# When a block-sum step's sums are rounded: before or after the next step's load work

## The chip, the cores and the metric

One core of a Trainium2 chip runs the whole kernel. The metric is the device time of one execution in microseconds (us). The engines are TensorE (PE for its matmuls, PEld for its weight loads), VectorE (DVE), ScalarE (ACT), GpSimd (POOL) and SyncE (SP), which issues most DMAs. Each takes its own instructions strictly in the order in which the program holds them, and waits on semaphores for the others.

## What is computed

The reference is a trunk of two residual layers on 256 tokens of 2048 features, all in float32: an attention mixer, then a recurrent mixer, each followed by a gated feed-forward of width 5632. The change touches the feed-forward alone:

```python
def swiglu(h, w_gate, w_up, w_down):
    return (jax.nn.silu(h @ w_gate) * (h @ w_up)) @ w_down

for i in range(DEPTH):          # DEPTH = 2
    ...
    x = x + swiglu(rms_norm(x, norm_ffn[i]), ffn_w_gate[i], ffn_w_up[i], ffn_w_down[i])
```

## The kernel before

**Products of float32.** A float32 operand is split in a rounded part `hi` (type fp32r) and a remainder `lo`, and a product takes three matmuls: hi by hi, hi by lo, lo by hi. Weights come from HBM as float32 tiles `raw`. ACT rounds `raw` to `hi` (L160), DVE subtracts to get `lo` (L164 or L173), and PE multiplies (L351).

**Steps.** `load_step` brings one step's weights, 1 MB: two half tiles of 128 x 1024 each, so its `hi` and its `lo` cost one 128 x 2048 instruction each. A plain step is eight products, 24 matmuls of 512 columns. A block-sum step covers the same part of the product as a plain step with seven products in place of eight, 21 matmuls. For it `load_step(True)` also makes three sums of weight blocks. One quarter of the tile arrives as a sum already, because POOL issues a DMA that adds to what SP's DMA wrote (L157). DVE then forms the others in place in `raw`, first one block (L166, 512 wide), then two (L167, 1024 wide). ACT rounds them to `wth` (L170, 512 and 1024 wide), and DVE takes the remainders `wtl` (L171, the same widths). PE's order in a block-sum step is four products from `hi` and `lo` (12 matmuls), then three from `wth` and `wtl` (9 matmuls). The first of these three takes the last of the three sums, so PE's 13th matmul needs the 1024 wide `wth` and the 14th the 1024 wide `wtl`.

**Groups.** A feed-forward is cut in parts of 12, 16 and 16 blocks of 128 hidden features. Each part has 3 or 4 gate/up units (512 columns of `w_gate` and of `w_up` each), then two pairs of column groups of `w_down`. Each unit or pair is a group of eight steps, called 0 to 7 here (six in the `w_down` pairs of the first part). Steps 1, 3 and 5 are block-sum steps (1 and 3 in the groups of six; 3 and 5 in a layer's first unit, whose steps run in the order 0, 1, 2, 4, 3, 6, 5, 7; none in the second `w_down` pair of layer 0's last part). The program has 93 of them. In a group of eight, steps 6 and 7 are loaded as two halves for each of the two column groups, so that the first column group is done before the second.

**What follows a gate/up unit.** When a unit's sums are done, DVE adds the parts (L851), ACT takes the SiLU (L618), DVE multiplies (L855) and transposes (L868). ACT then copies the 32 x 32 blocks into place with 16 instructions (L874), rounds the result to an operand of the down product (L881), DVE takes the remainder (L882), and where the down product will have a block-sum step there, DVE and ACT prepare its token sums (L333, L336, L337). All of this is queued in `owed`, and is emitted while the next group's steps 1 to 3 are: three pieces after step 1's loading (`settle(3)`).

**What sets the order.** PE's order is the order of the code. For ACT and DVE, `in_line` (L109) ties each engine's load work (L160, L164, L173, L166, L167, L170, L171) in the order in which it is written; a scheduler places the other instructions around it.

**Buffers.** `raw` has 4, `hi` and `lo` have 3 each, `wth` and `wtl` one each. So the rounding of a step waits until PE has finished the step three before it, the rounding of its sums until PE has finished the previous block-sum step, and a step's DMA until DVE is through with the `raw` of the step four before it.

Of the kernel before, what the change touches and what calls it, by code (L numbers as in the profile page):

```python
# [12 lines left out]
F32 = mybir.dt.float32  # L13
F32R = mybir.dt.float32r
AF = mybir.ActivationFunctionType
ALU = mybir.AluOpType
AX = mybir.AxisListType

P = 128
# [13 lines left out]
WIDE = 512  # L33
# [37 lines left out]
def trunk(ctx, tc, w, out):  # L71
    nc = tc.nc
    act, dve, pool, pe, sync = nc.scalar, nc.vector, nc.gpsimd, nc.tensor, nc.sync
# [13 lines left out]
    def nm(s):  # L87
        uid[0] += 1
        return f"{s}_{uid[0]}"
# [8 lines left out]
    def follow(i, j):  # L98
        tc.add_manual_dep(
            i.ins, j.ins.name,  # L100
            mybir.DependencyInfo(mybir.DependencyClass.NoSync, mybir.DependencyReason.DATA),
            reason="order",
        )
        return i
# [4 lines left out]
    def in_line(eng, i):  # L109
        if eng in line:  # L110
            if line[eng] is not None:
                follow(i, line[eng])
            line[eng] = i
        return i
# [6 lines left out]
    def settled(i, n, eng="dve"):  # L121
        for k in [k for k in due if k[0] <= n and k[1] == eng]:
            for j in due.pop(k):
                follow(i, j)

    def load_tiles():
        return [wp.tile([P, 2, HALF, P], dt, tag=t, name=nm(t), bufs=n) for t, dt, n in (("raw", F32, 4), ("hi", F32R, 3), ("lo", F32R, 3))]
# [17 lines left out]
            settled(rest, taken[0] - 1)  # L145
        return [(hi[:, i, :], lo[:, i, :]) for i in range(n)]

    def load_step(seven=False):
        assert taken[0] % 2 == 0
        srcs = [order[taken[0] + i][0] for i in range(2)]  # L150
        taken[0] += 2
        raw, hi, lo = load_tiles()
        if seven:
            for k in (1, 0):
                sl = slice(k * FOUR, k * FOUR + FOUR)
                sync.dma_start(out=square(raw[:, 1, sl, :]), in_=square(srcs[1][:, sl, :]))
            pool.dma_start(out=square(raw[:, 1, FOUR:, :]), in_=square(srcs[1][:, :FOUR, :]), accum_op=ALU.add)  # L157
        for i in range(1 if seven else 2):
            newest["load"] = sync.dma_start(out=raw[:, i], in_=srcs[i])
        newest["cast"] = in_line("act", act.copy(hi, raw))  # L160
        settled(newest["cast"], taken[0] - 1, "act")
        b = [t[:].rearrange("p j (k c) f -> p (j k) (c f)", k=2) for t in (raw, hi, lo)]
        if seven:
            settled(in_line("dve", dve.tensor_tensor(lo, raw, hi[:].bitcast(F32), ALU.subtract)), taken[0] - 1)  # L164
            t = b[0]
            in_line("dve", dve.tensor_tensor(t[:, 0, :], t[:, 3, :], t[:, 0, :], ALU.subtract))  # L166
            in_line("dve", dve.tensor_tensor(t[:, 1:3, :], t[:, 1:3, :], t[:, :1, :].broadcast_to([P, 2, WIDE]), ALU.subtract))  # L167
            th, tl = (fp[1].tile([P, 3, WIDE], F32R, tag=n, name=nm(n), bufs=1) for n in ("wth", "wtl"))
            for sl in (slice(0, 1), slice(1, 3)):
                in_line("act", act.copy(th[:, sl, :], t[:, sl, :]))  # L170
                in_line("dve", dve.tensor_tensor(tl[:, sl, :], t[:, sl, :], th[:, sl, :].bitcast(F32), ALU.subtract))  # L171
        else:
            settled(in_line("dve", dve.tensor_tensor(lo, raw, hi[:].bitcast(F32), ALU.subtract)), taken[0] - 1)  # L173
        w = [(b[1][:, i, :], b[2][:, i, :]) for i in range(4)]
        return w + [(th[:, i, :], tl[:, i, :]) for i in range(3)] if seven else w

    def halves(src, kt):
        return [(src[:, a : min(a + HALF, kt), :], min(HALF, kt - a)) for a in range(0, kt, HALF)]
# [61 lines left out]
    taken = [0]  # L240
# [34 lines left out]
    def step():  # L275
        clock[0] += 1
        due = [i for i, (t, _) in enumerate(waiting) if t <= clock[0]]
        if due:
            waiting.pop(due[0])[1]()
# [8 lines left out]
    def new_accs():  # L288
        return [new_acc() for _ in range(2)]
# [25 lines left out]
    def square(t):  # L315
        return t.rearrange("p c f -> p (c f)")
# [3 lines left out]
    def settle(n=1):  # L320
        while owed and n:
            owed.pop(0)()
            n -= 1
# [16 lines left out]
    def project_pair(xs, forms, plan, middle, done, ready=None, turned=True):  # L340
        banks, spare = [[], []], []
        begun = set()

        def bank(j, a):
            if not banks[j]:
                banks[j].extend(new_accs())
            return banks[j][a]

        def product(acc, x, wt, last=False):
            for i, (a, b) in enumerate(((x[0], wt[0]), (x[0], wt[1]), (x[1], wt[0]))):  # L350
                pe.matmul(acc, a, b, start=id(acc) not in begun, stop=last and i == 2)  # L351
                begun.add(id(acc))
            step()
            step()

        def tokens(k, a):
            return [xs[k][:, o + a * P : o + (a + 1) * P] for o in (0, S)]

        seven = [n for n, cols in plan if n in forms]
        for i, (n, cols) in enumerate(plan):  # L360
            if n in forms:
                s1, s2, s3, s4 = forms[n]
                b11, b21, b22, t3, t2, t4, t1 = load_step(True)
                settle(3)
                if n == seven[0]:
                    p1, q6, q5, q7 = (ps_m.tile([P, WIDE], F32, tag="pm", name=nm("pm")) for _ in range(4))
                last = n == seven[-1]
                product(p1, tokens(2 * n, 0), b11, last)
                product(bank(0, 0), tokens(2 * n + 1, 0), b21)
                product(bank(1, 0), s4, b22)  # L370
                product(q7, s3, t3, last)
                product(q5, s1, t1, last)
                product(q6, s2, t2, last)
                product(bank(0, 1), tokens(2 * n + 1, 1), t4)
                if last:
                    middle(p1, q5, q6, q7)
                continue
            if len(cols) == 1 and i and len(plan[i - 1][1]) == 2:
                settle(-1)
                if ready:  # L380
                    ready()
            end = n == plan[-1][0]
            for j in cols:
                if not spare:
                    w = load_step()
                    spare.extend((w[:2], w[2:]))
                w = spare.pop(0)
                if i:
                    settle(2 if len(owed) > 6 else 1)
                for a in range(2):  # L390
                    for k in range(2):
                        product(bank(j, a), tokens(2 * n + k, a), w[1 - k if turned and j else k], end and k == 1)
                if end:
                    done(j, banks[j])
# [163 lines left out]
    fp = []  # L558
# [16 lines left out]
    def output(xs, norm, ready):  # L575
        def done(c, accs):
            for a, acc in enumerate(accs):
                y = x_tok[:, a, c, :]
                not_after(dve.tensor_tensor(y, y, acc, ALU.add))
            norm.add(c)  # L580

        project_pair(xs, {}, pair_plan(range(KT // 2), READY), None, done, ready, False)
        for c in (2, 3):
            done(c, project_tokens(xs))


    def down(n, xs, forms, norm=None, end=False):
        for c in (0, 2):
            def middle(*banks):
                t = merge(*banks)  # L590
                y = x_tok[:, :, c : c + 2, :].rearrange("p a c f -> p c a f")
                dve.tensor_tensor(y, y, t, ALU.add)

            def done(j, accs):
                for a in range(2):
                    m = 2 if end and c + j == NCOL - 1 else 1
                    for i in range(m):
                        sl = slice(i * WIDE // m, (i + 1) * WIDE // m)
                        y = x_tok[:, a, c + j, sl]
                        not_after(dve.tensor_tensor(y, y, accs[a][:, sl], ALU.add))  # L600
                        if end:
                            sync.dma_start(out=out[:, a, c + j, sl], in_=y)
                if norm is not None:
                    norm.add(c + j)

            alone = norm is not None and c > 0
            project_pair(xs, {} if alone else forms, down_plan(n // 2, alone), middle, done)
# [525 lines left out]
```

## Time and profile before

| | |
|---|---|
| three runs | 2153.76, 2154.16, 2154.3 us; median 2154.16 |
| the profiled execution | 2155.09 us; its span, first to last instruction, 2153.3 us |
| busy over the span | PE 94%, DVE 80%, ACT 62%, POOL 9% |
| DMA | 410.48 MB, mean 191 GB/s |
| mean granted TensorE clock | 0.974 |

In rows of the trace a matmul of 512 columns shows as 0.39 us, but one starts every 0.227 us when PE does not wait, because they are pipelined. PE's busy time therefore hides short waits, and the time between starts tells more. Where a row has a bracket, the engine stood idle before it for so long, and the name behind the arrow ended the wait.

### The profile page before, as it was taken

Reading aid. Unit: us, or ns where it says so; the run is one execution under the profiler, and the core shown is the slowest. Engines: PE = TensorE matmul, PEld = TensorE weight load, DVE = VectorE, ACT = ScalarE, POOL = GpSimd, SP = SyncE. Lnnn points to the kernel's source line nnn. Section 1 sums busy time; section 2 is a strip of 40 time slices with the busy share of each in tenths; the row PEclk is TensorE's granted clock in tenths of the full one; section 3 lists DMA queues with packets and bytes.
Section 4 is the critical chain, followed back from the end, with each engine's and each line's share of the span. In section 5 each row is a group of like instructions: output and inputs, shape, how many; then the busy total and the mean of one; then the engine's idle time right before and its main releaser. Section 6 shows DMA issues by size and latency. Waiting matters only on the chain.

```text
span 2153.3 us, 26372 instructions
## 1 busy us (share of the span) xinstructions
PE 2030.9 (94%) x9641; PEld 1683.1 (78%) x9641; DVE 1724.3 (80%) x1928; ACT 1327.9 (62%) x1803; POOL 185.3 (9%) x240
## 2 busy tenths in 40 slices
PE   9999999899898998889999999998998999988999
PEld 7888877687777886668899998877787777877777
DVE  6777887797777887779888877877787777877778
ACT  6665765645565546667699996665555555555653
POOL 0011000000000000001033420000000000000000
PEclk9999999999999999999999999999999999999999
DMA  9533565576556775666555545656576565766565
GB/s 356 179 138 120 203 190 174 167 217 212 171 174 199 219 219 171 188 180 236 189 172 179 193 140 203 192 181 193 171 226 188 187 190 175 218 189 189 177 194 163
DMA packets 136354, 410.48 MB, mean 191 GB/s; under 512 B 15264, under 2 KB 16160, under 8 KB 135968
## 3 DMA queue, kind: packets, MB, share of 16 engines
q1 hardware_dynamic: 122688, 384.40, 52.2%
q0 software_dynamic: 13392, 24.39, 7.0%
q8 instruction: 75, 1.23, 0.2%
q14 instruction: 55, 0.45, 0.1%
q10 hardware_dynamic: 144, 0.02, 0.0%
HBM read 406.64 MB, written 2.10 MB: 190 GB/s over the span
## 4 chain that ended last, share of the span: by engine, by line
PE 58%; DVE 17%; ACT 16%; issue 6%; DMA 2%; POOL 0%; ACTq 0%; SPq 0%; DVEq 0%; POOLq 0%
PE acc L351 40%; PE acc L300 9%; PE pm L351 6%; ACT hi L160 6%; ACT tf L874 5%; DVE lo L173 3%; DVE raw L167 2%; DVE lo L164 2%; DVE fg L851 1%; DVE fg L855 1%; DVE raw L166 1%; DVE tb L868 1%; ACT L618 1%; ACT wth L170 1%; ACT sg L618 1%
## 5 line engine op out<-in xcount | busy, mean ns | idle before, releaser
L351 PE MATMUL acc<-hi,xg 128*128 128x512 f32 x1920 | 638.9, 404 | 28.0 <-ACT hi L160 28.0
L160 ACT CAST hi<-raw 128x2048 fp32r<-128x2048 f32 x280 | 528.1, 1907 | 139.4 <-DMA raw<-in_w_up_dram 50.0
L173 DVE TENSOR_TENSOR lo<-raw,hi 128x2048 fp32r<-128x2048 f32 x187 | 425.9, 2291 | 148.5 <-ACT hi L160 148.4
L351 PEld LDWEIGHTS acc<-hi,xg 128*128 128x128 f32 x1920 | 377.3, 197 | 114.4 <-ACT hi L160 34.9
L170 ACT CAST wth<-raw 128x512 fp32r<-128x512 f32 (+1 forms) x186 | 155.8, 837 | 442.1 <-DVE raw L166 362.2
L351 PE MATMUL acc<-lo,xg 128*128 128x512 f32 x960 | 392.6, 409 | 37.6 <-DVE lo L173 37.6
L351 PE MATMUL acc<-hi,act 128*128 128x512 f32 x1258 | 411.5, 398 | 11.5 <-ACT hi L160 10.5
L351 PEld LDWEIGHTS acc<-hi,act 128*128 128x128 f32 x1258 | 242.4, 193 | 64.7 <-ACT hi L160 13.1
L351 PE MATMUL acc<-lo,act 128*128 128x512 f32 x629 | 252.5, 401 | 14.2 <-DVE lo L173 14.0
L351 PEld LDWEIGHTS acc<-lo,xg 128*128 128x128 f32 x960 | 188.4, 196 | 89.6 <-DVE lo L173 50.2
L164 DVE TENSOR_TENSOR lo<-raw,hi 128x2048 fp32r<-128x2048 f32 x93 | 212.6, 2286 | 37.2 <-ACT hi L160 37.1
L171 DVE TENSOR_TENSOR wtl<-raw,wth 128x512 fp32r<-128x512 f32 (+1 forms) x186 | 177.4, 955 | 47.0 <-ACT wth L170 47.0
L144 DVE TENSOR_TENSOR lo<-raw,hi 128x1024 fp32r<-128x1024 f32 (+1 forms) x146 | 179.3, 1256 | 30.2 <-ACT hi L142 29.6
L142 ACT CAST hi<-raw 128x1024 fp32r<-128x1024 f32 (+1 forms) x146 | 145.0, 1035 | 41.1 <-PE acc L300 14.8
L351 PEld LDWEIGHTS acc<-lo,act 128*128 128x128 f32 x629 | 121.0, 192 | 44.8 <-DVE lo L173 20.5
L157 POOL DMA_DIRECT2D raw<-in_w_up_dram x64 | 55.5, 867 | 1054.1 <-DMA raw<-in_w_up_dram 911.4
L406 PE MATMUL acc<-xg,hi 128*128 128x256 f32 x512 | 145.6, 284 | 0.0
L407 PE MATMUL acc<-xg,hi 128*128 128x256 f32 x512 | 145.4, 284 | 0.0
L408 PE MATMUL acc<-xg,lo 128*128 128x256 f32 x512 | 145.1, 283 | 0.0
L874 ACT COPY tf<-tb 32x256 f32<-32x256 f32 x352 | 141.6, 402 | 4.1
L167 DVE TENSOR_TENSOR raw<-raw 128x1024 f32<-128x1024 f32 x93 | 113.0, 1215 | 2.4
L300 PE MATMUL acc<-hi,xg 128*128 128x512 f32 x320 | 107.8, 397 | 0.7 <-ACT hi L142 0.7
(208 smaller groups left out, 3162.7 us busy)
## 6 DMA issues: line engine op xcount, KB each, us to landing
raw<-in_w_gate_dram SPq DMA_DIRECT2D x176, 512.0 KB, 4.7
raw<-in_w_down_dram SPq DMA_DIRECT2D x147, 512.0 KB, 5.0
raw<-in_w_up_dram SPq DMA_DIRECT2D x112, 512.0 KB, 4.9
raw<-in_w_up_dram SPq DMA_DIRECT2D x128, 256.0 KB, 3.2
raw<-in_w_in_dram SPq DMA_DIRECT2D x64, 512.0 KB, 4.7
raw<-in_w_qkv_dram SPq DMA_DIRECT2D x46, 512.0 KB, 5.9
raw<-in_w_o_dram SPq DMA_DIRECT2D x32, 512.0 KB, 4.0
raw<-in_w_up_dram POOLq DMA_DIRECT2D x64, 256.0 KB, 6.1
```

The lines of the kernel that those rows point to most:

```text
L144: rest = in_line("dve", dve.tensor_tensor(lo[:, sl, :], raw[:, sl, :], hi[:, sl, :].bitcast(F32), ALU.subtract))
L160: newest["cast"] = in_line("act", act.copy(hi, raw))
L164: settled(in_line("dve", dve.tensor_tensor(lo, raw, hi[:].bitcast(F32), ALU.subtract)), taken[0] - 1)
L167: in_line("dve", dve.tensor_tensor(t[:, 1:3, :], t[:, 1:3, :], t[:, :1, :].broadcast_to([P, 2, WIDE]), ALU.subtract))
L170: in_line("act", act.copy(th[:, sl, :], t[:, sl, :]))
L171: in_line("dve", dve.tensor_tensor(tl[:, sl, :], t[:, sl, :], th[:, sl, :].bitcast(F32), ALU.subtract))
L173: settled(in_line("dve", dve.tensor_tensor(lo, raw, hi[:].bitcast(F32), ALU.subtract)), taken[0] - 1)
L300: pe.matmul(accs[a], x, wt[:, k, :], start=(k0 + k == 0 and n == 0), stop=(end and k == 1 and n == 2))
L351: pe.matmul(acc, a, b, start=id(acc) not in begun, stop=last and i == 2)
L406: pe.matmul(o, hi, x[:, :S], start=start, stop=False)
L407: pe.matmul(o, hi, x[:, S:], start=False, stop=False)
L874: n = act.copy(f[32 * i : 32 * i + 32, q::4, :, :], b[32 * q : 32 * q + 32, :, i, :, :])
```

## The change

`load_step` is split. `begin_step` issues a step's DMAs, its `hi` and its `lo`, and for a block-sum step also the two subtractions in `raw`. The new `load_step`, when it is asked for a block-sum step, first calls `begin_step` for the step behind it and keeps the result in `begun`; only then come the roundings `wth` and the remainders `wtl` of its own sums. No instruction is added or removed. PE's order, and that of the DMAs on SP and POOL, is the same as before; on ACT and on DVE the order differs around each of the 93 block-sum steps.

```diff
+    begun = []
+
+    def begin_step(seven):
...
         newest["cast"] = in_line("act", act.copy(hi, raw))
         settled(newest["cast"], taken[0] - 1, "act")
+        settled(in_line("dve", dve.tensor_tensor(lo, raw, hi[:].bitcast(F32), ALU.subtract)), taken[0] - 1)
...
         if seven:
-            settled(in_line("dve", dve.tensor_tensor(lo, raw, hi[:].bitcast(F32), ALU.subtract)), taken[0] - 1)
             in_line("dve", dve.tensor_tensor(t[:, 0, :], t[:, 3, :], t[:, 0, :], ALU.subtract))
             in_line("dve", dve.tensor_tensor(t[:, 1:3, :], t[:, 1:3, :], t[:, :1, :].broadcast_to([P, 2, WIDE]), ALU.subtract))
+        return t, [(hi[:, i, :], lo[:, i, :]) for i in range(4)]
+
+    def load_step(seven=False, after=False):
+        t, w = begun.pop() if begun else begin_step(seven)
+        if not seven:
+            return w
+        begun.append(begin_step(after))
+        hi, lo = (fp[1].tile([P, 3, WIDE], F32R, tag=n, name=nm(n), bufs=1) for n in ("wth", "wtl"))
+        for sl in (slice(0, 1), slice(1, 3)):
+            in_line("act", act.copy(hi[:, sl, :], t[:, sl, :]))
+            in_line("dve", dve.tensor_tensor(lo[:, sl, :], t[:, sl, :], hi[:, sl, :].bitcast(F32), ALU.subtract))
+        return w + [(hi[:, i, :], lo[:, i, :]) for i in range(3)]
...
-                b11, b21, b22, t3, t2, t4, t1 = load_step(True)
+                b11, b21, b22, t3, t2, t4, t1 = load_step(True, plan[i + 1][0] in forms)
```

The next two pairs show one group of the first layer, the third gate/up unit, from step 1's rounding on. On ACT before, `raw_3193` is step 1's tile, `raw_3246` step 2's, `raw_3285` step 3's, `raw_3334` step 4's; L874 are the 16 copies of the unit before:

```order
L160 CAST hi_3194<-raw_3193 128x2048
L618 ACTIVATE fg_3082<-fg_3082,nr_2503 128x512
L170 CAST wth_3204<-raw_3193 128x512
L170 CAST wth_3204<-raw_3193 128x1024
L874 COPY tf_3211<-tb_3210 32x2x128 x8
L160 CAST hi_3247<-raw_3246 128x2048
L874 COPY tf_3211<-tb_3210 32x2x128 x8
L160 CAST hi_3286<-raw_3285 128x2048
L881 CAST act_3302<-tf_3211 128x4x256
L336 CAST hf_537_3310<-tb_3305 128x512
L170 CAST wth_3296<-raw_3285 128x512
L170 CAST wth_3296<-raw_3285 128x1024
```

On ACT now, at the same place (`raw_3204` is step 2's tile, `raw_3296` step 4's; code below the change stands five lines lower):

```order
L162 CAST hi_3194<-raw_3193 128x2048
L623 ACTIVATE fg_3089<-fg_3089,nr_2503 128x512
L162 CAST hi_3205<-raw_3204 128x2048
L178 CAST wth_3211<-raw_3193 128x512
L178 CAST wth_3211<-raw_3193 128x1024
L879 COPY tf_3218<-tb_3217 32x2x128 x16
L162 CAST hi_3286<-raw_3285 128x2048
L162 CAST hi_3297<-raw_3296 128x2048
L886 CAST act_3309<-tf_3218 128x4x256
L341 CAST hf_540_3317<-tb_3312 128x512
L178 CAST wth_3303<-raw_3285 128x512
L178 CAST wth_3303<-raw_3285 128x1024
```

Step 2's rounding moved from the middle of the 16 copies to a place ahead of step 1's sums, and step 4's rounding ahead of step 3's sums.

On DVE before, from step 1's second subtraction on:

```order
L167 TENSOR_TENSOR raw_3193<-raw_3193 128x1024
L171 TENSOR_TENSOR wtl_3205<-raw_3193,wth_3204 128x512
L171 TENSOR_TENSOR wtl_3205<-raw_3193,wth_3204 128x1024
L173 TENSOR_TENSOR lo_3248<-raw_3246,hi_3247 128x2048
L333 TENSOR_TENSOR tb_3305<-tf_3211 128x128 x2
L333 TENSOR_TENSOR tb_3305<-tf_3211,tb_3305 128x128 x2
L164 TENSOR_TENSOR lo_3287<-raw_3285,hi_3286 128x2048
L882 TENSOR_TENSOR act_3302<-tf_3211,act_3302 128x4x256
L337 TENSOR_TENSOR hf_537_3310<-tb_3305,hf_537_3310 128x512
L166 TENSOR_TENSOR raw_3285<-raw_3285 128x512
L167 TENSOR_TENSOR raw_3285<-raw_3285 128x1024
L171 TENSOR_TENSOR wtl_3297<-raw_3285,wth_3296 128x512
```

On DVE now, from the same instruction on:

```order
L168 TENSOR_TENSOR raw_3193<-raw_3193 128x1024
L164 TENSOR_TENSOR lo_3206<-raw_3204,hi_3205 128x2048
L179 TENSOR_TENSOR wtl_3212<-raw_3193,wth_3211 128x512
L179 TENSOR_TENSOR wtl_3212<-raw_3193,wth_3211 128x1024
L338 TENSOR_TENSOR tb_3312<-tf_3218 128x128 x2
L338 TENSOR_TENSOR tb_3312<-tf_3218,tb_3312 128x128 x2
L164 TENSOR_TENSOR lo_3287<-raw_3285,hi_3286 128x2048
L167 TENSOR_TENSOR raw_3285<-raw_3285 128x512
L887 TENSOR_TENSOR act_3309<-tf_3218,act_3309 128x4x256
L168 TENSOR_TENSOR raw_3285<-raw_3285 128x1024
L164 TENSOR_TENSOR lo_3298<-raw_3296,hi_3297 128x2048
L342 TENSOR_TENSOR hf_540_3317<-tb_3312,hf_540_3317 128x512
```

Step 2's remainder (`lo_3206`) moved ahead of the remainders of step 1's sums, and step 4's (`lo_3298`) ahead of those of step 3's sums, which come next, behind L342.

More of the change, by code (lines that the diff above doesn't have):

```diff
@@ L146, in load_half @@
         return [(hi[:, i, :], lo[:, i, :]) for i in range(n)]
-    def load_step(seven=False):
+    begun = []
+    def begin_step(seven):
         assert taken[0] % 2 == 0
@@ L161, in load_step @@
         settled(newest["cast"], taken[0] - 1, "act")
-        b = [t[:].rearrange("p j (k c) f -> p (j k) (c f)", k=2) for t in (raw, hi, lo)]
+        settled(in_line("dve", dve.tensor_tensor(lo, raw, hi[:].bitcast(F32), ALU.subtract)), taken[0] - 1)
+        t, hi, lo = (t[:].rearrange("p j (k c) f -> p (j k) (c f)", k=2) for t in (raw, hi, lo))
         if seven:
-            settled(in_line("dve", dve.tensor_tensor(lo, raw, hi[:].bitcast(F32), ALU.subtract)), taken[0] - 1)
-            t = b[0]
             in_line("dve", dve.tensor_tensor(t[:, 0, :], t[:, 3, :], t[:, 0, :], ALU.subtract))
             in_line("dve", dve.tensor_tensor(t[:, 1:3, :], t[:, 1:3, :], t[:, :1, :].broadcast_to([P, 2, WIDE]), ALU.subtract))
[L168 to L175, printed above, removed]
+        return t, [(hi[:, i, :], lo[:, i, :]) for i in range(4)]
[9 more added lines that the diff above has]
+        return w + [(hi[:, i, :], lo[:, i, :]) for i in range(3)]
     def halves(src, kt):
```

## The prediction, made before the change was run

> **What bounds the kernel now.** I read first the page's busy times, then what PE waited for, then stretches of one group.
>
> ```profile
> PE 2030.9 (94%) x9641; PEld 1683.1 (78%) x9641; DVE 1724.3 (80%) x1928; ACT 1327.9 (62%) x1803; POOL 185.3 (9%) x240
> PE acc L351 <- DVE lo L173: 51.6, 43, 1.8
> PE acc L351 <- ACT hi L160: 38.5, 22, 1.8
> PE pm L351 <- DVE wtl L171: 22.1, 38, 0.8
> ...
> 359.40:409.70 50.30, 44.81 (x184) 35.26 (x183) 39.32 (x38) 29.41 (x35) 2.58 (x3) 0.97 0.59 183
> ...
> 480.90:522.50 41.60, 41.60 (x185) 34.33 (x184) 35.23 (x30) 21.22 (x17) 2.60 (x3) 1.00 0.70 221
> ```
>
> PE is the busiest, and what it waits for is always a rounding (`hi`) or a remainder (`lo`, `wtl`). The last two rows (start:end, length, then busy times of PE, PEld, DVE, ACT, POOL, granted clock, DMA) are two groups of the same eight steps, each from one group's step 1 to the next one's. The second stands behind a `w_down` pair and runs at PE's own pace. The first stands behind a gate/up unit and takes 8.7 us more. There are 22 gate/up units, so some 190 us of the span lie in such groups. By step, the first of the two:
>
> ```profile
> 359.40:366.90 7.50, 5.22 (x22) 3.68 (x20) 3.10 (x4) 6.08 (x10) 0.28 (x1) 1.00 0.38 112
> 366.90:376.20 9.30, 7.44 (x24) 5.83 (x25) 7.32 (x9) 6.58 (x11) 0.58 (x1) 0.82 0.60 164
> 376.20:382.40 6.20, 5.37 (x22) 3.87 (x21) 5.07 (x5) 4.94 (x4) 0.00 (x0) 1.00 0.18 35
> 382.40:388.70 6.30, 5.79 (x26) 4.47 (x25) 5.72 (x6) 2.19 (x4) 0.00 (x0) 1.00 0.80 302
> 388.70:393.40 4.70, 4.70 (x22) 3.90 (x21) 4.11 (x3) 4.70 (x4) 0.21 (x1) 1.00 0.50 173
> ```
>
> The last row is a block-sum step without a wait: 4.7 us, 21 matmuls 0.227 us apart; 24 of them, a plain step, are 5.45. Against that step 1 loses 2.8 us, step 2 3.9, step 3 1.5, step 4 0.85. ACT's queue and DVE's show where the losses come from:
>
> ```profile
> 358.44 0.62 ACT L170 CAST wth<-raw 128x512 fp32r<-128x512 f32 x1 [5.34 <-DVE raw L166]
> 360.70 1.05 ACT L170 CAST wth<-raw 128x1024 fp32r<-128x1024 f32 x1 [1.64 <-DVE raw L167]
> 361.66 3.31 ACT L874 COPY tf<-tb 32x256 f32<-32x256 f32 x8
> 364.99 1.90 ACT L160 CAST hi<-raw 128x2048 fp32r<-128x2048 f32 x1
> 366.91 3.29 ACT L874 COPY tf<-tb 32x256 f32<-32x256 f32 x8
> 370.23 1.90 ACT L160 CAST hi<-raw 128x2048 fp32r<-128x2048 f32 x1
> 372.03 1.04 ACT L881 CAST act<-tf 128x1024 fp32r<-128x1024 f32 x1
> 372.98 0.62 ACT L336 CAST hf<-tb 128x512 fp32r<-128x512 f32 x1
> ...
> 359.49 1.18 DVE L167 TENSOR_TENSOR raw<-raw 128x1024 f32<-128x1024 f32 x1
> 360.59 0.68 DVE L171 TENSOR_TENSOR wtl<-raw,wth 128x512 fp32r<-128x512 f32 x1
> 361.79 1.23 DVE L171 TENSOR_TENSOR wtl<-raw,wth 128x1024 fp32r<-128x1024 f32 x1 [0.52 <-ACT wth L170]
> 366.92 2.29 DVE L173 TENSOR_TENSOR lo<-raw,hi 128x2048 fp32r<-128x2048 f32 x1 [3.91 <-ACT hi L160]
> ...
> 372.16 2.29 DVE L164 TENSOR_TENSOR lo<-raw,hi 128x2048 fp32r<-128x2048 f32 x1 [0.90 <-ACT hi L160]
> 374.37 1.22 DVE L882 TENSOR_TENSOR act<-tf,act 128x1024 fp32r<-128x1024 f32 x1
> 375.50 0.69 DVE L337 TENSOR_TENSOR hf<-tb,hf 128x512 fp32r<-128x512 f32 x1
> 376.11 0.69 DVE L166 TENSOR_TENSOR raw<-raw 128x512 f32<-128x512 f32 x1
> ...
> 377.97 0.68 DVE L171 TENSOR_TENSOR wtl<-raw,wth 128x512 fp32r<-128x512 f32 x1
> 379.17 1.23 DVE L171 TENSOR_TENSOR wtl<-raw,wth 128x1024 fp32r<-128x1024 f32 x1 [0.52 <-ACT wth L170]
> 380.97 2.29 DVE L173 TENSOR_TENSOR lo<-raw,hi 128x2048 fp32r<-128x2048 f32 x1 [0.57 <-ACT hi L160]
> ```
>
> Step 2's rounding (364.99) stands behind eight of the copies. Step 3's `wtl` ends at 380.40, step 4's `lo` at 383.26, and until then PE is fed by this chain; behind it the group runs free. So the group's length is decided by the ends of step 3's `wtl` and step 4's `lo`; what PE loses in steps 1 and 2 costs nothing more.
>
> **Removed and moved.** No instruction goes; the question is when this chain ends. I walk it in the new order on the same clock. The starts above give DVE's pace when it does not wait: a `lo` every 2.2 us (372.16 to 374.37), a 1024 wide one 1.13, a 512 wide one 0.6.
>
> Step 1: its second subtraction starts at 359.49. At 360.59 now comes step 2's `lo`, whose rounding ACT can do in the 5.34 us ahead of 358.44 that it now spends waiting. The `wtl` start at 362.8 and 363.4 and end at 364.6. PE wants the last one with its 14th matmul, at 359.40 + 13 x 0.227 = 362.35, so it stands 2.3 us. Eight more matmuls after it, the step ends near 366.6, and step 2 runs without a wait to 372.1 (now 376.2).
>
> Step 3: the 16 copies run together from 361.66, 3.33 + 3.32 us, to 368.3. Step 3's rounding ends at 370.2, step 4's at 372.0, L881 at 373.0. DVE: step 3's `lo` 370.25, L166 372.45, L882 373.05, L167 374.2, step 4's `lo` 375.3, L337 377.5, the `wtl` 378.1 and 378.7, their end 379.95. That is 0.45 us ahead of 380.40, and step 4's `lo` is done by then, so step 4's 0.85 goes as well. **Credit: 1.3 us in each of 22 groups, 29 us**; six of them have no L333 to L337, which brings both orders forward by the same 0.6.
>
> But PE now stands in another way. It ends step 3's first 12 matmuls at about 375.1, gets `wth` at 376.5 (L167 ends 375.4, plus 1.05) for one matmul, and `wtl` at 380.0. That is 4.7 us with one matmul, where now no wait is longer than 1.8 us (the last number of the rows of PE's waits). What standing does to the clock is in this trace, cut into stretches of 3.41 us in which the granted clock (third number from the end) is constant:
>
> ```profile
> 365.87:369.29 3.42, 0.53 (x2) 0.21 (x2) 2.29 (x1) 3.34 (x7) 0.86 (x1) 1.00 0.75 189
> 369.29:372.70 3.41, 3.41 (x8) 2.74 (x9) 1.53 (x5) 3.36 (x5) 0.00 (x0) 0.50 0.93 261
> ...
> 413.67:417.08 3.41, 1.85 (x8) 1.16 (x7) 0.00 (x0) 3.35 (x5) 0.00 (x0) 1.00 0.77 252
> 417.08:420.49 3.41, 1.38 (x5) 0.95 (x6) 2.29 (x1) 3.30 (x9) 0.00 (x0) 1.00 0.16 60
> 420.49:423.90 3.41, 3.41 (x10) 2.65 (x9) 1.39 (x1) 2.91 (x3) 0.00 (x0) 0.50 0.84 308
> ...
> 580.92:587.74 6.82, 5.03 (x12) 4.01 (x13) 4.86 (x6) 6.03 (x10) 0.00 (x0) 0.50 0.75 216
> ```
>
> A stretch with 2 or 5 matmuls is followed by one at half clock, one with 8 by full clock; a half-clock stretch that itself holds much standing is followed by another (the last row is two). At half clock a full stretch loses 3.41/2 = 1.7 us. Now these stretches lie in step 2, ahead of the `wtl` that everything waits for, and cost nothing. In the new order they lie behind that `wtl`, where PE is the bound. [...]
>
> The price, by where the stretches' borders fall. [...]
>
> The arithmetic of it: a stretch with 5 matmuls or fewer has 2.2 us of standing, so the last one that halves the clock ends between 2.2 us ahead of 380.0 and 1.2 behind. What is left of the half-clock stretch after 380.0 costs 0.6 to 1.7 us, on average 1.3, and in four of ten places a second follows, so 2.0. Where step 1's 2.3 us already halve the clock, again some four of ten, step 2 ends 1.7 later, the second standing is shorter, and I put it at 1.2. **Debit: 1.7 us in each of 22 groups, 37 us**; ends 0.6 (the tail of one stretch) and 2.4 (one whole and 0.7 of a second).
>
> Groups behind a `w_down` pair have no copies and no wait now, but the `lo` put ahead costs them too:
>
> ```profile
> 479.32 1.23 DVE L167 TENSOR_TENSOR raw<-raw 128x1024 f32<-128x1024 f32 x1
> 480.46 0.68 DVE L171 TENSOR_TENSOR wtl<-raw,wth 128x512 fp32r<-128x512 f32 x1
> 481.66 1.23 DVE L171 TENSOR_TENSOR wtl<-raw,wth 128x1024 fp32r<-128x1024 f32 x1 [0.52 <-ACT wth L170]
> ...
> 483.85 0.39 PE L351 MATMUL pm<-wtl,nf 128*128 128x512 f32 x1
> ```
>
> `wtl` ends at 482.89, 0.96 ahead of PE's need at 483.85. With a 2.2 us `lo` put in at 480.46 and the 0.52 us wait gone it ends at 480.46 + 2.2 + 0.6 + 1.23 = 484.5, so PE stands 0.65, 0.7 with the restart. Steps 3 and 5 have more slack there, since DVE no longer waits for ACT. Nine groups begin so (four in the first layer, five in the second), the chain is tied to PE's last sums by L600, and nothing gives it back: **6 us** more; the ends are 0 (DVE early by half a microsecond) and 9.
>
> Nothing else has a price. The longer hold on `raw` delays the DMA of the step four further on, with POOL's adding DMA behind it, by 1.6 us (364.6 for 363.0); PE takes that step at 388.70, 24 us later. SP's and POOL's own order stays. ACT's new place for step 2's rounding waits for PE's end of the step three before it, one plain step before 359.40, so at 354.0, four microseconds before the sums can be rounded at 358.44. The units that start a layer, attention and the recurrent mixer keep their slack.
>
> **The sum.** Profiled execution 2155.09 (span 2153.3 and 1.8 around it), 0.9 above the median 2154.16. 2155.1 - 29 + 37 + 6 = 2169, on the scale of the median 2168.
>
> **The rivals.**
> 1. *The half clock falls in the shadow* (faster). If the borders mostly fall early in step 3's standing, most of the half-clock stretch is over by the `wtl`, and each group pays 0.6: 22 x (1.3 - 0.6) = 15 gained, 6 paid, 2145. It decides for faster as soon as the mean price is under 1.0. For it: each group's length sets where the next one meets the borders, so places need not be even. Against: a second stretch follows when the first holds more standing. Chance 0.15.
> 2. [...] Chance 0.07.
> 3. *The two cancel*: a price near 1.0, or a `wtl` that ends some 0.4 us earlier than in my walk: 2154, within 4. Chance 0.16.
> 4. *The change doesn't bring step 2's rounding forward*, because its DMA is late. Then ACT's copies stand behind it too and the chain ends up to 1.9 us later, 2154 + 42 + 6 = 2202. The tile before it is in place far ahead in the row 364.99, which has no wait. Chance 0.02.
>
> The forecast, slower by some 14 us, has 0.60. A measurement of this kernel can tell about 0.2%, 4.3 us, from no change. The range of 8 in 10 goes from 2145 (rival 1) to 2184 (price 2.4). Slower by over 0.2%: 0.62; same 0.16; faster 0.22.
>
> **What would show it.** Right: PE's waits for `lo` and `hi` (90 us together) fall to under 25; those for `wtl` rise from 22 to some 90 with a longest of about 3 us, and new ones for `wth` appear; step 2 is 5.5 us long where the clock is full; half-clock stretches lie from step 3's last matmuls into step 4; ACT's wait ahead of `wth` shrinks; step 1 behind a `w_down` pair stands about 0.6. Wrong: groups near 49 us with full clock in step 4; step 3's `wtl` ending more than half a microsecond away from 20.5 us after step 1's start; no standing at 480.9's place.

## The result, and the profile after

| | us, median (runs) | ratio to before, 95% interval | span of the profiled execution | mean granted clock |
|---|---|---|---|---|
| before | 2154.23 (2153.76 to 2155.08) | | 2153.3 | 0.974 |
| changed | 2169.82 (2168.54 to 2170.80) | 1.0072 [1.0054, 1.0089] | 2168.2 | 0.972 |

The changed kernel is slower by 15.6 us; 13.8 were forecast. The page's busy times of the changed kernel and the rows of what PE waited for (us in total, times, longest; below the change the lines stand 5 further down than before):

```profile
PE 2022.5 (93%) x9641; PEld 1684.1 (78%) x9641; DVE 1713.5 (79%) x1928; ACT 1332.1 (61%) x1803; POOL 182.6 (8%) x240
PE pm L356 <- DVE wtl L179: 113.7, 53, 3.0
PE pm L356 <- ACT wth L178: 19.1, 16, 1.3
...
PE pm L356 <- DVE lo L164: 1.3, 8, 0.2
...
PE acc L356 <- DVE lo L164: 0.9, 1, 0.9
```

The waits for `lo` and `hi`, 90 us before, have all but gone. Those for `wtl` grew from 22 to 114, and `wth` is new. Whole groups come next, from one step 1 to the next: two behind a gate/up unit, and in the middle one behind a `w_down` pair.

```profile
359.50:410.80 51.30, 44.79 (x185) 35.63 (x184) 39.06 (x38) 29.39 (x35) 2.58 (x3) 0.93 0.58 180
483.50:525.80 42.30, 41.78 (x184) 34.28 (x183) 34.74 (x30) 21.79 (x17) 2.60 (x3) 1.00 0.70 218
525.80:575.00 49.20, 43.98 (x184) 35.33 (x183) 39.02 (x38) 29.49 (x35) 2.59 (x3) 0.97 0.58 187
359.50:366.70 7.20, 5.05 (x22) 3.87 (x21) 5.24 (x5) 5.74 (x13) 0.51 (x1) 1.00 0.31 96
366.70:372.20 5.50, 5.50 (x26) 4.51 (x24) 2.81 (x5) 5.43 (x8) 0.35 (x1) 1.00 0.99 298
372.20:383.80 11.60, 7.25 (x22) 4.98 (x21) 11.50 (x11) 6.58 (x6) 0.00 (x0) 0.74 0.44 148
383.80:389.70 5.90, 5.90 (x26) 4.80 (x25) 4.53 (x4) 1.58 (x2) 0.00 (x0) 0.93 0.53 175
389.70:394.50 4.80, 4.80 (x23) 3.98 (x22) 2.67 (x2) 4.24 (x3) 0.86 (x1) 1.00 0.98 297
```

The last five rows are steps 1 to 5 of the first group. Step 2 now runs without a wait (5.5 us for 9.3), and step 3 takes 11.6 for 6.2, at a clock of 0.74, which goes on into step 4 (0.93). The group is 51.3 us long, where it was 50.3; the group behind a `w_down` pair 42.3, where it was 41.6; and the third, also behind a gate/up unit, only 49.2. On ACT and then DVE, the same group:

```profile
354.33 1.92 ACT L162 CAST hi<-raw 128x2048 fp32r<-128x2048 f32 x1 [2.90 <-issue]
358.57 0.62 ACT L178 CAST wth<-raw 128x512 fp32r<-128x512 f32 x1 [2.32 <-DVE raw L167]
...
361.79 6.62 ACT L879 COPY tf<-tb 32x256 f32<-32x256 f32 x16
368.43 3.73 ACT L162 CAST hi<-raw 128x2048 fp32r<-128x2048 f32 x2
...
360.72 2.28 DVE L164 TENSOR_TENSOR lo<-raw,hi 128x2048 fp32r<-128x2048 f32 x1
362.92 1.81 DVE L179 TENSOR_TENSOR wtl<-raw,wth 128x512 fp32r<-128x512 f32 x2
...
370.38 2.29 DVE L164 TENSOR_TENSOR lo<-raw,hi 128x2048 fp32r<-128x2048 f32 x1 [0.91 <-ACT hi L162]
...
375.58 2.28 DVE L164 TENSOR_TENSOR lo<-raw,hi 128x2048 fp32r<-128x2048 f32 x1
377.78 0.68 DVE L342 TENSOR_TENSOR hf<-tb,hf 128x512 fp32r<-128x512 f32 x1
378.38 1.82 DVE L179 TENSOR_TENSOR wtl<-raw,wth 128x512 fp32r<-128x512 f32 x2
```

Step 2's rounding fills ACT's old wait (354.33). The roundings of steps 3 and 4 follow the sixteen copies (368.43), and step 4's `lo` (375.58) stands in front of step 3's `wtl`, whose second half ends at 378.38 + 1.82 = 380.2. What that standing does to the clock, in stretches on the borders of the granted clock: four of this group, then four of the group that is 49.2 us long.

```profile
374.38:377.79 3.41, 1.68 (x7) 0.79 (x5) 3.41 (x4) 2.09 (x2) 0.00 (x0) 1.00 0.00 0
377.79:381.21 3.42, 0.95 (x2) 0.83 (x3) 3.42 (x5) 2.55 (x2) 0.00 (x0) 0.50 0.64 213
381.21:384.62 3.41, 3.41 (x9) 2.63 (x8) 3.34 (x4) 0.50 (x1) 0.00 (x0) 0.50 1.00 370
384.62:388.03 3.41, 3.41 (x16) 2.79 (x15) 3.41 (x3) 1.08 (x2) 0.00 (x0) 1.00 0.25 53
...
528.00:531.40 3.40, 1.24 (x6) 0.74 (x5) 3.05 (x3) 3.32 (x9) 0.00 (x0) 1.00 0.25 83
531.40:534.80 3.40, 3.40 (x9) 2.63 (x8) 0.06 (x1) 3.28 (x10) 0.86 (x1) 0.50 0.90 301
...
541.60:545.00 3.40, 1.89 (x8) 1.00 (x6) 3.40 (x4) 3.00 (x3) 0.00 (x0) 1.00 0.00 0
545.00:548.40 3.40, 1.84 (x8) 1.54 (x9) 3.40 (x3) 1.65 (x1) 0.00 (x0) 1.00 0.92 318
```

In the first group two stretches at half clock follow step 3's standing, the second of them full of work behind the `wtl`. In the other group it is step 1's standing (528.00) that halves the clock, while PE would have to wait for the chain in step 3 anyway, so a slower step 2 costs nothing. Step 2 then ends later, step 3's standing begins later, its stretches hold 8 matmuls each, and the clock stays full. So the same cost can fall on the path or beside it.

### The profile page after: what moved, and what is told of

Its sections match the earlier page's. It is cut to its first block, busy times and chain, and to the rows that moved or that the text cites. A ratio compares the mean times of both kernels' runs of the same rounds, so it can differ in the third digit from the quotient of the medians.

```text
span 2168.2 us, 26518 instructions
## 1 busy us (share of the span) xinstructions
PE 2022.5 (93%) x9641; PEld 1684.1 (78%) x9641; DVE 1713.5 (79%) x1928; ACT 1332.1 (61%) x1803; POOL 182.6 (8%) x240
## 3 DMA queue, kind: packets, MB, share of 16 engines
q1 hardware_dynamic: 122688, 384.40, 51.8%
## 4 chain that ended last, share of the span: by engine, by line
PE 58%; DVE 19%; ACT 12%; issue 9%; DMA 2%; POOL 0%; DVEq 0%; SPq 0%; ACTq 0%; POOLq 0%
PE acc L356 37%; PE acc L305 9%; PE pm L356 8%; DVE lo L164 6%; ACT tf L879 5%; DVE wtl L179 3%; DVE raw L168 2%; ACT hi L162 2%; DVE raw L167 2%; DVE fg L856 1%; DVE fg L860 1%; ACT L623 1%; DVE lo L144 1%; ACT sg L623 1%; DMA graw<-in_w_gates_dram 1%
## 5 line engine op out<-in xcount | busy, mean ns | idle before, releaser
L356 PE MATMUL acc<-hi,xg 128*128 128x512 f32 x1920 | 618.3, 392 | 0.0
L356 PEld LDWEIGHTS acc<-hi,xg 128*128 128x128 f32 x1920 | 365.6, 190 | 77.9
L356 PE MATMUL acc<-hi,act 128*128 128x512 f32 x1258 | 404.9, 392 | 1.6 <-DVE hv L696 0.9
L356 PE MATMUL acc<-lo,xg 128*128 128x512 f32 x960 | 376.5, 392 | 0.0
L356 PE MATMUL acc<-lo,act 128*128 128x512 f32 x629 | 246.3, 392 | 0.9 <-DVE lo L164 0.9
L356 PEld LDWEIGHTS acc<-lo,xg 128*128 128x128 f32 x960 | 182.8, 190 | 38.8
L142 ACT CAST hi<-raw 128x1024 fp32r<-128x1024 f32 (+1 forms) x146 | 145.0, 1036 | 42.6 <-PE acc L305 14.8
L179 DVE TENSOR_TENSOR wtl<-raw,wth 128x512 fp32r<-128x512 f32 (+1 forms) x186 | 169.2, 950 | 0.0
L356 PE MATMUL pm<-wtl,nf 128*128 128x512 f32 x128 | 60.2, 470 | 84.0 <-DVE wtl L179 84.0
L856 DVE TENSOR_TENSOR fg<-acc,fg 128x512 f32<-128x512 f32 x88 | 60.7, 689 | 77.5 <-PE acc L356 77.3
L356 PE MATMUL pm<-wth,nf 128*128 128x512 f32 x256 | 101.6, 440 | 13.4 <-ACT wth L178 12.8
```

Source lines behind the costliest of these rows:

```text
L142: newest["cast"] = in_line("act", act.copy(hi[:, sl, :], raw[:, sl, :]))
L179: in_line("dve", dve.tensor_tensor(lo[:, sl, :], t[:, sl, :], hi[:, sl, :].bitcast(F32), ALU.subtract))
```

## The experiments

All kernels do the same computation. The matmuls of zeros in some of them add nothing to a sum; they keep PE occupied where it stands. "Fed" groups are the 22 behind a gate/up unit. Each ratio is to executions of the kernel before that were measured beside it (their medians are 2154.1 to 2155.2 us). The last four columns split one trace of each kernel, whose time is up to 3.2 us away from the median: the lengths of the 22 fed groups added up (by the starts of the first matmuls of step 1), their difference from before divided by 22, then what the nine groups behind a `w_down` pair, and all the rest of the span, differ from before.

| kernel | us, median | ratio, 95% interval | 22 fed groups | per fed group | nine groups | rest |
|---|---|---|---|---|---|---|
| before | | | 1084.0 | | | |
| changed | 2169.82 | 1.0072 [1.0054, 1.0089] | 1092.0 | +0.37 | +6.2 | +0.5 |
| changed, zeros in steps 1 and 3 | 2140.74 | 0.9928 [0.9914, 0.9941] | 1058.7 | -1.15 | +6.2 | +6.9 |
| before, zeros in steps 2 and 3 | 2160.32 | 1.0025 [1.0014, 1.0036] | 1084.9 | +0.04 | +0.4 | +5.5 |
| new order not in fed groups | 2162.62 | 1.0032 [1.0020, 1.0043] | 1084.0 | 0.00 | +6.7 | -1.6 |
| new order in fed groups only | 2170.08 | 1.0069 [1.0056, 1.0082] | 1097.1 | +0.60 | -0.6 | +0.1 |
| the same, zeros in steps 1 and 3 | 2134.40 | 0.9906 [0.9891, 0.9922] | 1058.8 | -1.14 | -0.6 | +6.8 |
| changed, zeros in step 3 alone | 2144.11 | 0.9951 [0.9939, 0.9964] | 1061.7 | -1.01 | +6.2 | +5.6 |
| changed, zeros in step 1 alone | 2187.99 | 1.0154 [1.0140, 1.0168] | 1110.8 | +1.22 | +6.2 | +1.0 |
| changed, the tile of zeros unused | 2169.89 | 1.0069 [1.0056, 1.0081] | 1093.4 | +0.43 | +6.2 | -0.4 |
| only the rounding ahead | 2097.55 | 0.9735 [0.9722, 0.9749] | 1024.7 | -2.70 | -1.2 | -0.3 |
| new order in the fed groups' step 1 alone | 2115.87 | 0.9822 [0.9809, 0.9836] | 1046.1 | -1.72 | 0.0 | -1.0 |
| only the rounding ahead, zeros in step 3 | 2087.76 | 0.9689 [0.9676, 0.9703] | 1017.6 | -3.02 | -1.2 | +0.2 |

**Is the half clock the debit?** The theory of the prediction: the new order shortens the chain, and the half clock, moved behind it, costs more than that. The rival: the new order costs by its chain and the clock only goes with it. The standing was filled with matmuls by a tile of zeros (`ident` less itself), in the changed kernel and, at its own places, in the order before. `fed` is true behind a gate/up unit.

```diff
+        def fill(acc, n):
+            for _ in range(n):
+                pe.matmul(acc, zero[0], xs[0], start=False, stop=False)
...
                 product(q7, s3, t3, last)
+                if fed and seven.index(n) < 2:
+                    fill(*((q5, 17) if seven.index(n) else (q7, 9)))
                 product(q5, s1, t1, last)
```

For the order before, 15 such matmuls stand at the start of step 2, in `bank(0, 0)`, and 11 in step 3, in `q5`.

> The changed kernel, with matmuls by a tile of zeros put into the two places where PE stands behind a gate/up unit: 9 in step 1 (2.0 us) and 17 in step 3 (3.9 us), ahead of the product that waits for the last remainder. They add nothing to the sums. Theory (the half clock behind the standing is the price): the chain to step 3's wtl ends where it did, some 20.7 us after step 1's start, but the clock stays full in steps 1 to 4, the fed groups are 49.0 us long where most are now 51, and the time is 2154 - 29 + 6 = 2131, within 5. Rival (the new order costs through the length of its chain, the clock only goes with it): clock full, groups still 51, time 2170 or more. If both share it, about 2150.

> The order of the kernel before, with the matmuls of zeros put where PE stands in that order behind a gate/up unit: 15 at the start of step 2 (3.4 us), 11 in step 3 (2.5 us). Theory (before, the half clock lies ahead of step 3's wtl, in the shadow of the chain): the granted clock in step 2 rises from 0.82 to near 1, and the time stays 2154, within 4. Rival (the half clock costs before as well, 1.7 us a stretch in 22 groups): 2154 - 37 = 2117; then the debit of the change cannot be the clock that it moves.

A fed group of each, by windows: first the changed kernel with the filling, group and step 3, then the order before with it.

```profile
357.80:407.00 49.20, 48.29 (x210) 38.99 (x209) 38.98 (x38) 29.52 (x35) 2.58 (x3) 1.00 0.61 188
...
370.40:380.40 10.00, 9.21 (x40) 6.93 (x39) 9.97 (x9) 6.70 (x7) 0.00 (x0) 1.00 0.37 119
```

```profile
358.70:409.10 50.40, 48.60 (x210) 38.91 (x209) 39.33 (x38) 29.45 (x35) 2.58 (x3) 1.00 0.59 183
```

DVE's rows for step 3's last `wtl` in these two groups, in the same order:

```profile
376.68 1.82 DVE L182 TENSOR_TENSOR wtl<-raw,wth 128x512 fp32r<-128x512 f32 x2
...
378.50 1.23 DVE L182 TENSOR_TENSOR wtl<-raw,wth 128x1024 fp32r<-128x1024 f32 x1 [0.52 <-ACT wth L181]
```

The chain has not moved: it ends 378.5 - 357.8 = 20.7 us after step 1's start in the changed order and 379.7 - 358.7 = 21.0 in the order before, with the filling as without it. What the filling changes is the clock. In the changed order the filling takes 33.3 us off the fed groups (1092.0 to 1058.7). In the order before it takes nothing off: the clock goes from 0.82 in step 2 to 1.00 in the whole group, and the group stays 50.4 us long. So the half clock was in the shadow before and on the path after, and the rivals (2170 for the first kernel, 2117 for the second) fall. At full clock in both, the new order gains 1084.9 - 1058.7 = 26 us in these groups. The changed kernel with the filling came out 10 us above the expectation, and 7 of them lie outside the groups (the last column). The order before with the filling, at 2160.3, missed its 2154, within 4, as well, and there 5.5 us lie outside the groups; more on that below.

**Where does the loss lie?** The order was made to depend on what stands ahead of the group.

```diff
+AHEAD = lambda fed, k: not fed
...
-        begun.append(begin_step(after))
+        if ahead:
+            begun.append(begin_step(after))
```

The second kernel has `fed` in place of `not fed`.

> The new order only where no copies run beside it (groups behind a w_down pair, and units that start a layer), the order before in the 22 fed groups. Theory: the remainder put ahead makes PE stand 0.65 us in step 1 of nine groups, 6 us in all: 2160, within 3. Rival 1 (that standing is made up later): 2154, same. Rival 2 (most of the loss of the change is here and not in the fed groups): 2165 to 2170.

> The new order only in the 22 groups behind a gate/up unit. Theory: 22 x (1.7 - 1.3) = 9 us more, 2163, within 4, and with the nine other groups' 6 us the whole loss of 15.6. Rival 1 (credit and debit cancel in these groups, the loss comes from the others): 2154. Rival 2 (all the loss lies here): 2170.

In the first of these kernels the nine groups cost 6.7 us, as expected, and nothing gives it back. The second missed its expectation: 2170.1 for 2163, within 4, which is the time of its rival 2. The reason is not that rival's, since the nine groups do cost their 6.2 us in the changed kernel: the fed groups cost 13.2 alone, more than the 8.1 that they cost there. The parts don't add up, since the groups meet the borders of the clock at other places: in the changed kernel five fed groups get away without a price (four of 49.2 us, and the one from 1526.0, which is as long as with the filling), here only one does.

**Which standing costs?** The filling of one step alone, and, last, the tile of zeros made and not used.

```diff
-                if fed and seven.index(n) < 2:
+                if fed and seven.index(n) == 1:
```

For step 1 alone the condition is `== 0`, with 9 into `q7`.

> The changed kernel with the 17 matmuls of zeros in step 3 alone; step 1 stands as in the changed kernel. Theory (only the half clock that step 3's standing brings costs; the one that step 1 brings falls into step 2 and is covered by step 3's wait): most fed groups 49.2 us; where step 2 runs at half clock the filling itself ends up to 1 us late in about a third of them: 2142 to 2150. Rival (both standings cost alike): about half of the gain, 2155.

> The changed kernel with the 9 matmuls of zeros in step 1 alone; step 3 stands. Theory: nothing halves the clock early any more, so step 3's standing does it in every fed group, the seven groups of 49.2 us are gone and all are near 51: 2170 to 2178, no gain at all although a standing of 2.3 us is filled 22 times. Rival (both standings cost alike): 2155.

> The changed kernel with the tile of zeros made and never used: a control for the 6 us that the stretch between the layers (recurrent mixer) was longer in both runs with the matmuls of zeros. If making or placing the tile does it: 2176. If the matmuls do it by the time at which the stretch begins, or if that stretch only wanders from build to build: 2170, within 3.

With step 3 alone filled, the fed groups are 48.6 to 49.4 us (38.4 for the two groups of six steps): step 1's standing still halves the clock in half of them, 11 of 22, and that costs up to 0.2, in two groups 0.8 (the filling itself, queued behind a slower step 2, ends that much later; up to 1 us was expected). With step 1 alone filled the kernel is 18 us slower than with no filling at all. A fed group of it, and three stretches in it:

```profile
360.90:412.50 51.60, 47.11 (x194) 37.58 (x193) 39.00 (x38) 29.38 (x35) 2.58 (x3) 0.93 0.56 179
...
376.48:379.89 3.41, 0.93 (x3) 0.19 (x1) 3.41 (x4) 2.83 (x3) 0.00 (x0) 1.00 0.00 0
379.89:383.31 3.42, 1.69 (x4) 1.41 (x5) 3.42 (x3) 1.82 (x2) 0.00 (x0) 0.50 0.79 305
383.31:386.72 3.41, 3.41 (x9) 2.67 (x9) 3.34 (x4) 1.23 (x2) 0.00 (x0) 0.50 0.82 309
```

Every one of the 22 groups now has such a pair of stretches at half clock, and its price is (1110.8 - 1058.7)/22 = 2.4 us. The sign was as expected, the size was not (2188 for at most 2178): a second stretch had been expected in some groups and came in all. So a halving in step 1 costs little and is mostly a cover: it delays work that has time, and shortens step 3's standing, which has none.

**Which half of the change makes which effect?** By the walk, the credit comes from the rounding put ahead, and the standing from the remainder put ahead, which takes DVE 2.2 us in front of the last `wtl`. In the first of these kernels the next step's rounding alone goes ahead, and its remainder follows the sums' `wtl`. The third adds 10 matmuls of zeros in step 3 to that. The second has the changed order in step 1 of the fed groups alone.

```diff
         newest["cast"] = in_line("act", act.copy(hi, raw))
         settled(newest["cast"], taken[0] - 1, "act")
+        return raw, hi, lo
+
+    def end_step(seven, raw, hi, lo):
         settled(in_line("dve", dve.tensor_tensor(lo, raw, hi[:].bitcast(F32), ALU.subtract)), taken[0] - 1)
...
-        t, w = begun.pop() if begun else begin_step(seven)
+        early = begun.pop() if begun else begin_step(seven)
+        t, w = early if len(early) == 2 else end_step(seven, *early)
```

> Half of the change, without matmuls of zeros: only the next step's rounding is put ahead of a block-sum step's sums, its remainder stays behind the last wtl. Theory (the rounding ahead is the credit; the remainder ahead, 2.2 us of DVE in front of the last wtl, makes PE stand and with it the half clock): step 3's wtl ends 18.6 us after step 1's start instead of 20.7 and 21.0, step 4's lo at 20.8 instead of 23.9 before, so a fed group is 47.3 us at full clock; standing of 2.5 us in step 3 halves the clock in about half of the groups, 0.8 a group. Groups behind a w_down pair are 41.6 as before. 2155 - 22 x (3.0 - 0.8) = 2107, from 2090 to 2125. Rival (the credit needs the remainder ahead too): near 2155 or above.

> The change's order in step 1 of the fed groups alone, the order before in their steps 3 and 5 and everywhere else. Theory (the remainder ahead in step 3 is the harmful part): step 1's wtl late as in the changed kernel, step 3's wtl ends 18.6 us after step 1's start, step 4's rounding runs behind its wth and step 4's lo ends at 21.2, a group is 47.7 at full clock and 0.8 longer with the half clock: 2155 - 22 x (2.6 - 0.8) = 2115, from 2100 to 2130. Rival (it is the standing in step 1 that costs): 2160 to 2170.

> The kernel with only the rounding ahead, and 10 matmuls of zeros (2.3 us) in step 3 of the fed groups. Theory: full clock, fed groups 47.3 us: 2155 - 66 = 2089, and 2095 if the stretch between the layers is again 6 us longer. Rival (no half clock is left in that order): the same time as without the matmuls of zeros.

The kernel with only the rounding ahead: what PE waited for, then a fed group and one behind a `w_down` pair by windows, then DVE's rows and one of ACT's.

```profile
PE pm L365 <- DVE lo L169: 34.9, 22, 1.6
PE pm L365 <- DVE wtl L188: 29.2, 44, 0.8
PE pm L365 <- ACT wth L187: 28.2, 22, 1.3
```

```profile
356.20:403.40 47.20, 43.05 (x185) 33.99 (x184) 39.13 (x38) 29.55 (x35) 2.58 (x3) 1.00 0.62 195
...
473.10:514.50 41.40, 41.40 (x184) 34.30 (x183) 34.84 (x30) 21.59 (x17) 2.60 (x3) 1.00 0.73 222
```

```profile
358.58 1.23 DVE L188 TENSOR_TENSOR wtl<-raw,wth 128x1024 fp32r<-128x1024 f32 x1 [0.52 <-ACT wth L187]
359.73 2.29 DVE L169 TENSOR_TENSOR lo<-raw,hi 128x2048 fp32r<-128x2048 f32 x1
...
367.05 2.29 DVE L169 TENSOR_TENSOR lo<-raw,hi 128x2048 fp32r<-128x2048 f32 x1 [0.92 <-ACT hi L164]
...
372.86 1.82 DVE L188 TENSOR_TENSOR wtl<-raw,wth 128x512 fp32r<-128x512 f32 x2
374.59 4.49 DVE L169 TENSOR_TENSOR lo<-raw,hi 128x2048 fp32r<-128x2048 f32 x2
...
365.10 3.71 ACT L164 CAST hi<-raw 128x2048 fp32r<-128x2048 f32 x2
```

Step 3's `wtl` ends at 372.86 + 1.82 = 374.7, 18.5 us after step 1's start (20.7 in the changed kernel), and step 4's `lo` comes behind it. The longest wait is 1.6 us instead of 3.0, the group behind a `w_down` pair pays nothing, and a fed group is 47.2 us. The filling in the third kernel takes another 7 us off the fed groups, so a half clock was left in some of them: four fed groups are 48.5 to 48.6 us long in the first kernel instead of 47.2, and one of six steps is 38.4 instead of 37.0. All three times are within 10 us of what was expected. In the first, 5 of 22 groups paid for a half clock where half of them were put in. The second, 2115.9 for 2115, is so near by luck: at full clock its groups are 48.4 us long and not 47.7, and only three pay for a half clock behind step 3's standing. The first of these beats both kernels without an added instruction, at 0.9735 [0.9722, 0.9749].

**The best of the old theory**, put down before the last three kernels were run:

> The best version the theory points to: the new order only in the 22 fed groups, with the matmuls of zeros in their steps 1 and 3, the order before elsewhere. From the runs so far: fed groups 49.2 instead of 50.3 us (25 less in all), groups behind a w_down pair 41.6 as before, so 2155 - 25 = 2130, and up to 2136 if the stretch between the layers is again 6 us longer, as in the two other runs with the matmuls of zeros. Rival (part of the gain hung on the phase that the slower groups set): 2140 and more.

It came to 2134.4, with 25 us gained in the fed groups and the rest of the span again 6.8 us longer.

## Why the prediction was right, point by point

**The credit**, forecast as 29 us. At full clock the fed groups gained 25 to 26, in the runs with the filling. The walk had the two ends right: step 3's `wtl` came at 380.2 in the group whose step 1 starts at 359.5, so 20.7 after it, where 20.55 was forecast and 21.0 was the kernel before; and step 4's `lo` was out of the way. 0.3 + 0.85 = 1.15 us a group instead of 1.3. The 0.15 too much comes from DVE's steps, which take a little longer than walked: counted from step 1's start, step 3's `lo` stands at 10.88 for 10.85, step 4's `lo` at 16.08 for 15.9, the first `wtl` at 18.88 for 18.7.

**The debit**, forecast as 37 us, 1.7 a group. Removing the half clock took off 33.3 us, 1.5 a group. The mechanism is as forecast: step 3's `wtl` ends 20.7 us after step 1's start in every fed group with token sums (20.1 in the six without), with the half clock and without it, so the whole price is the clock behind it. That the size is so near is partly luck. In 15 groups, where step 3's standing met a full clock, the price was 1.6 to 2.4, on average 1.94 (forecast 2.0). In the other seven step 1's standing halved the clock first. There the prediction took 1.2 and it was 0 in five groups and 1.7 and 2.6 in two, 0.6 on average; and they were 7 of 22, not four in ten. The averages in the debit (1.3, and four of ten places) count all places of the borders alike, which no run shows: filling step 1 brought the mean of all 22 groups to the upper end, 2.4 us, since the groups then meet the borders of the clock in nearly the same place each time (the half clock begins 18.3 to 19.8 us after step 1's start in every one). A mean over even places is not what this kernel, with groups of nearly equal length, met.

**Groups behind a `w_down` pair**, forecast as 6 us from 0.65 of standing: DVE and PE in the changed kernel.

```profile
483.09 2.29 DVE L164 TENSOR_TENSOR lo<-raw,hi 128x2048 fp32r<-128x2048 f32 x1
485.29 1.82 DVE L179 TENSOR_TENSOR wtl<-raw,wth 128x512 fp32r<-128x512 f32 x2
...
486.25 0.39 PE L356 MATMUL pm<-wth,nf 128*128 128x512 f32 x1
487.17 0.50 PE L356 MATMUL pm<-wtl,nf 128*128 128x512 f32 x1 [0.52 <-DVE wtl L179]
```

The matmul for `wtl` starts 0.92 behind the one before it, where 0.227 is the pace: 0.69 of standing. Nine groups gave 6.2 us, and 6.7 where they alone had the new order. The term stands.

**The sum**: -25.2 + 33.3 + 6.2 + 0.5 = 14.8 between the two spans, for the forecast -29 + 37 + 6 = 14. Credit and debit were each forecast some 4 us too large, and the two errors cancel. How much of the agreement is luck the other kernels show: with the tile of zeros made and not used the debit is 34.7 us, with the new order in the fed groups alone 38.3, with step 1 filled 52.1, all for the same order in these groups.

**The rivals.** The half clock in the shadow (rival 1) is real: it happened in five groups out of 22, which show the prediction's sign of being wrong, a length near 49 us and full clock in step 4. It came by another way than written: through step 1's standing, not through where the border falls in step 3's. That was too few to turn the sign. How many they are depends on where the groups meet the borders: with the new order in the fed groups alone there was one, and those groups cost 13.2 us instead of 8.1. Rival 2, no half clock and the whole credit kept, is refuted by the rows above: with no wait over 3.0 us the clock halves in all 22 fed groups, in 17 of them behind step 3's standing. Without a half clock the 33 us that the filling took off would not be there. (The prediction's 1.8 us for the longest wait in the order before holds in the feed-forwards; elsewhere PE has one of 2.1 us.) Rival 3, that the two cancel within 4 us, is outside the measured interval, which begins at 1.0054, 11.6 us. Rival 4 (the rounding late by its DMA) fell with the row at 354.33, which has no DMA ahead of it.

**What was not foreseen** is that the two halves of the change pull apart. The walk held the reason in it: step 4's `lo`, 2.2 us of DVE, stands ahead of step 3's `wtl`, and PE takes it only with step 4, from 383.8. Without it the same walk gives a `wtl` 2.2 us sooner, and the kernel is 2.65% faster instead of 0.7% slower.

**Left open.** In four of the six kernels with matmuls of zeros the rest of the span was 5.5 to 6.9 us longer. In the first of them 6.7 us of it lie in the recurrent mixer between the layers (239.1 us before, 245.8 there), where ACT waits for the gates' weights; before, and with the filling:

```profile
ACT ghi L945 <- DMA graw<-in_w_gates_dram: 2.3, 5, 0.8
```

```profile
ACT ghi L962 <- DMA graw<-in_w_gates_dram: 10.3, 9, 2.0
```

The tile alone doesn't do it (-0.4), nor does filling as such (+0.2 in the kernel with only the rounding ahead, +1.0 with step 1 alone). What does was not tried. It is left out of the readings above, which go by the groups.

## What to carry to other kernels

When an order is changed so that several results come earlier, walk each of them separately to the one that the end waits for: here the rounding had an idle engine to run in, while the remainder went in front of the critical subtraction on a full one, and only the first was worth moving. Before a standing is priced, ask in which stretch of the clock its consequence falls; in these runs a slow stretch ahead of the thing that all wait for cost up to 0.2 us, in two groups 0.8 (step 3 alone filled), and the slow stretches behind it 2.4 us a group (step 1 alone filled). Where one cost seems to be the clock, filling the standing with work that changes nothing, in both orders, separates the clock from the chain in two runs.

## What the runs showed of the hardware

- The clock of a stretch of 3.41 us went with the number of matmuls in the one before it, more finely than the prediction's rows show: stretches with 6 and 7 (528.00, 374.38) were followed by half clock, those with 8 (541.60, 545.00) by full clock. In the feed-forwards of all thirteen traces, counted in the same way (every matmul that touches the stretch), full-clock stretches with up to 6 were always followed by half clock and those with 8 or more always by full clock; 7 went either way, 22 times to half clock and 16 times to full. The same number held in a stretch at half clock, where 8 to 10 were counted where PE was busy throughout (8 at 369.29 and 10 at 420.49 in the kernel before): with 2 or 4 (377.79 and 379.89) the next was at half clock again, with 9 (381.21) it was full, and in all the traces up to 6 were always followed by half clock and 8 or more by full. So a half-clock stretch with 6 matmuls or fewer was always followed by another; in the changed kernel 10 of the 25 times at half clock that end within the span are such pairs, 6.83 us long.
- The borders lie on one grid through the whole execution: the starts of the half-clock stretches in the changed kernel, from 330.0 to 2166.4, are multiples of 3.4133 us apart (538 of them between these two), within 0.02 us. In each of the thirteen executions the grid begins at another place, 0.3 to 3.1 us behind the first instruction. So in these traces the grid goes on through every change of the work, and where it lies differs from one execution to the next (0.65 us behind the first instruction before, 2.30 in the changed kernel). Fifteen stretches are 51.2 us, close to the length of a fed group that pays for a half clock (50.8 to 51.8 for those of eight steps in the changed kernel), so neighbouring groups often meet the grid in nearly the same place.
